# The FFN's down product by one level of Strassen's method, one product of halves at a time

## The chip, the core and the metric

The program runs on one core of one Trainium2 chip. The metric is the device time of one execution in microseconds, lower is better. The core has a matrix engine (PE, with its weight loads PEld), a vector engine (DVE), a scalar engine (ACT), a general engine (POOL) and a queue engine (SP); each works through its own list of instructions in order. DMAs are issued from SP's list (queue q1) and from POOL's list (queue q0).

## What is computed

One decoder layer for 1024 prompt rows and 64 sample rows with the same weights. The change concerns the last part, the convolutional feed-forward block:

```python
def conv_ffn(h, conv_buf, w_a, w_b, conv_w, conv_b, w_d):
    T = h.shape[1]
    a = h @ w_a                                    # (T, 4096)
    ctx = jnp.concatenate([conv_buf.astype(a.dtype), a], axis=1)
    c = conv_b
    for j in range(CONV_W):
        c = c + ctx[:, j:j + T] * conv_w[j]
    y = (jax.nn.silu(c) * (h @ w_b)) @ w_d         # (T, 4096) @ (4096, 1024)
    return y, ctx[:, -(CONV_W - 1):]
```

The result is normalised by row, scaled, and added to the residual. All values are float32 and the products have to be accurate, so each operand x is split into a high part (x rounded to fp32r) and a low part (the rest), and a product takes three matmuls: high with high, low with high, high with low.

## The kernel before, in words

The program is written with a tile framework that sets the order of the instructions on each engine before the run, from a simulated timeline; buffers come from pools, and an instruction that takes a buffer waits for its last reader.

**Stages.** Up to about 1630 us: attention, recurrence and the projections. From 1630 to 2337 us the up products (`up`, line 1609, and `ffn`, line 1653): the 4096 hidden columns go in 32 blocks of 128 (`fb`), two blocks at a time as a *pair*, 16 pairs. For a pair, `up` runs once for w_a and once for w_b, and it already uses the seven products of Strassen's method (Winograd's form, table `PRODS`): the 1024 model columns are the inner dimension in two halves, the two blocks are the two row halves, and the activation rows the two column halves. DVE makes the weight sums (line 1587), ACT and DVE the high and low parts (`split`, lines 143 and 144), and DVE and ACT take the results out of PSUM (lines 1635 to 1649, 1683 to 1685, 1705 to 1708). Between the two `up`s come the convolution (lines 1697 to 1699) and SiLU. The pair's hidden values stand in `ct`, tiles named `ext`, and POOL's queue writes them to memory (`yd`, lines 1711 and 1712), the 1024 prompt columns and the 64 sample columns of each block apart. In the same list POOL copies the convolution's tails (lines 1692 and 1693).

**The down product** (from 2337 us): `down_first` prepares blocks 0 and 1 during the last `up`; `down_group` (line 1769) then takes the blocks in groups: 1, 1, 2 and then seven groups of 4. For each of 8 row tiles of 128 prompt rows and each half of the 1024 output columns it runs 3 matmuls per block into a PSUM bank (line 1787) and adds the bank to an accumulator in SBUF (line 1793, DVE; for the first block lines 149 and 151). The sample rows' high and low parts are one 128-column stationary operand with 4 matmuls per block (line 1779). Each group's `w_d` rows and hidden values are loaded and split while the group before it runs (`prep`, line 1805; `down_part`, line 1735). In the last group each row tile is finished as soon as its sums are complete (`rows_done`, line 1818): residual loaded, row norm, scale, add, store.

**What sets the order around the change.** Six PSUM banks rotate in `down_bank`; PE's list is in program order up to what the simulated timeline moves; POOL's list carries the stores of the hidden values; SP's list carries all loads, and an SP entry that waits holds up those behind it.

Of the kernel before, what the change touches and what calls it, by code (L numbers as in the profile page):

```python
# [17 lines left out]
F32 = mybir.dt.float32  # L18
# [53 lines left out]
def _constants():  # L72
# [26 lines left out]
    for B in (2, 4, 8, 16, 32, 64):  # L99
# [7 lines left out]
RATES = (("prompt", 0.6), ("sample", 0.7), ("combine", 0.25))  # L107
RATE_INPUTS = 1.0
# [8 lines left out]
         ("S1", "T1", "C", True), ("A22", "T4", "B", False), ("S4", "B22", "C", False))  # L117


class Builder:  # L120
# [1265 lines left out]
    def phase3(self, early):  # L1386
# [3 lines left out]
        with ExitStack() as es:  # L1390
# [3 lines left out]
            self.yd = [self.dr.tile([P, NT], F32, name=f"yd{f}") for f in range(NFB)]  # L1394
# [258 lines left out]
    def ffn(self, es, eu, pool, fs, stT):  # L1653
# [5 lines left out]
        fp = pool(eu, "fp", 4)  # L1659
        W = SEQ + 2 + SB * 10  # L1660
# [9 lines left out]
        first_down = self.down_first(fp)  # L1670
        self.aside = chain(self.aside, first_down)
        for i in range(NFB // 2):
# [13 lines left out]
            self.up(store_a, i == 0)  # L1686
            ct = []
# [21 lines left out]
            self.up(store_b)  # L1709
            for m, fb in enumerate(fbs):  # L1710
                nc.gpsimd.dma_start(self.yd[fb][:, :SEQ], ct[m][:, 2:2 + SEQ])
                nc.gpsimd.dma_start(self.yd[fb][:, SEQ:].rearrange("p (b t) -> p b t", t=8), samples(ct[m])[:, :, 2:])
# [3 lines left out]
        for _ in range(2):  # L1716
            self.down_group([self.aready.popleft()])
        tails = fp.tile([P, W], F32, name="ext")
        o = 0
        for (j0, n, dst) in ((0, 2, O["p_ffn_conv"][0, 0]), (2, 16, O["s_ffn_conv"][0].rearrange("b j f -> (b j) f"))):  # L1720
            d2 = dst.rearrange("j (r p) -> (j r) p", p=P)
            for a in range(0, n, 4):
                w = min(4, n - a)
                ps = self.down_bank()
# [6 lines left out]
        self.down(es, pool)  # L1731
# [3 lines left out]
    def down_part(self, fb, raw, w, yraw, y, ys):  # L1735

        nc = self.nc
        nc.sync.dma_start(raw, self.I["w_ffn_d"][0][fb * P:(fb + 1) * P])
        nc.sync.dma_start(yraw, self.yd[fb])
        self.split(*w, raw)  # L1740
        self.split(*y, yraw[:, :SEQ])
        self.split(ys[:, 0], ys[:, 1], yraw[:, SEQ:])
        return w, y, ys.rearrange("p a b -> p (a b)")

    def wtile(self, pool, name, dt=F32R, bufs=2):
        return pool.tile([P, 8, P], dt, name=name, bufs=bufs).rearrange("p a f -> p (a f)")

    def down_first(self, fp):

        for fb in range(2):  # L1750
            w = [self.wtile(self.wp, n) for n in ("w_hi", "w_lo")]
            y = [self.wtile(self.uw, *n) for n in ((("wx", F32R, 3), ("wx", F32R, 3)), (("wx", F32R, 3), ("w_raw", F32R, 1)))[fb]]
            yraw = fp.tile([P, SEQ + 2 + SB * 10], F32, name="ext")[:, :NT]
            ys = self.uw.tile([P, 4, P], F32R, name="S", bufs=3)[:, 0].rearrange("p (a b) -> p a b", a=2)
            yield self.down_part(fb, self.wtile(self.wp, "w_raw", F32), w, yraw, y, ys)

    def down_start(self, pc):
        self.pc, self.nb = pc, 0
        accs = [self.actp.tile([P, 4, D], F32, name=f"act_{x}0") for x in "hl"]
        self.acc = [accs[i // 4][:, i % 4] for i in range(SEQ // P)]  # L1760
        self.smp = [pc.tile([P, 512], F32, name="ps_c") for _ in range(2)]
        self.ndown = 0

    def down_bank(self, n=6):
        pl, nm = [(self.pd, "ps_d"), (self.pu, "ps_u"), (self.pc, "ps_c")][(self.nb // 2) % (n // 2)]
        self.nb += 1
        return pl.tile([P, 512], F32, name=nm)

    def down_group(self, grp, after=lambda i: None, sampled=lambda: None):

        nc = self.nc
        G = len(grp)
        first = self.ndown == 0
        self.ndown += G
        last = self.ndown == NFB
        for k, (w, _, ys) in enumerate(grp):
            for u in range(2):
                for x in range(2):
                    nc.tensor.matmul(self.smp[u], ys, w[x][:, u * 512:(u + 1) * 512], start=first and k + x == 0, stop=last and k + x == G)  # L1779
        sampled()  # L1780
        for i, acc in enumerate(self.acc):
            for u in range(2):
                ps = self.down_bank()
                m = 0
                for w, y, _ in grp:
                    for a, b in ((0, 0), (1, 0), (0, 1)):
                        nc.tensor.matmul(ps, y[a][:, i * P:(i + 1) * P], w[b][:, u * 512:(u + 1) * 512], start=m == 0, stop=m == 3 * G - 1)  # L1787
                        m += 1
                dst = acc[:, u * 512:(u + 1) * 512]
                if first:  # L1790
                    self.copy(dst, ps)
                else:
                    nc.vector.tensor_add(dst, dst, ps)
            after(i)

    def down(self, es, pool):
# [3 lines left out]
        nc.sync.dma_start(gb, I["norm_ffn_post"][0].partition_broadcast(P))  # L1800
        sel = dp.tile([P, NS], F32, name="sel")
        nc.vector.tensor_add(sel, self.ident[:, :NS], self.ident[:, NS:])
        held = {}

        def prep(g, j, fb):

            if g % 2 == 0:
                if j == 0:
                    held[g] = [self.actp.tile([P, 4, D], F32R, name=f"act_{x}1") for x in "hl"]
                y = tuple(t[:, j] for t in held[g])  # L1810
            else:
                y = tuple(dp.tile([P, D], F32R, name=n, bufs=4) for n in ("yh", "yl"))
            w = (self.wtile(self.wp, "w_hi"), self.wtile(self.wp, "w_lo")) if g % 2 == 0 and j < 2 else \
                tuple(dp.tile([P, D], F32R, name="wd", bufs=12) for _ in range(2))
            ys = dp.tile([P, 2, NS], F32R, name="ys", bufs=9)
            return self.down_part(fb, self.wtile(self.wp, "w_raw", F32), w, dp.tile([P, NT], F32, name="y_raw", bufs=2), y, ys)

        def rows_done(src, rows, r0, dst):

            x, y = (dp.tile([P, D], F32, name=n, bufs=4)[:rows] for n in ("yh", "yl"))  # L1820
            nc.sync.dma_start(x, self.x1d[r0:r0 + rows])
            ss = self.sm.tile([P, 2], F32, name="pn_ss")[:rows]
# [3 lines left out]
            r = self.rstd(ss[:, 0:1], rows, D)  # L1826
            for u in range(2):
                v = slice(u * 512, (u + 1) * 512)
                nc.vector.scalar_tensor_tensor(y[:, v], src(u), r, gb[:rows, v], op0=ALU.mult, op1=ALU.mult)
                nc.vector.tensor_add(y[:, v], y[:, v], x[:, v])  # L1830
                nc.sync.dma_start(dst[:, v], y[:, v])

        def samples_done():
            s = [dp.tile([P, 512], F32, name=f"smp{u}") for u in range(2)]
            fin = []
            for u in range(2):
                nc.scalar.activation(s[u], self.smp[u], AF.Copy)
                ps = self.down_bank(4)[:NS]
                nc.tensor.matmul(ps, sel, s[u], start=True, stop=True)
                fin.append(ps)  # L1840
            rows_done(lambda u: fin[u], NS, SEQ, O["y_sample"].rearrange("b t d -> (b t) d"))
        groups = [(2, 3)] + [tuple(range(a, a + 4)) for a in range(4, NFB, 4)]
        grp = [prep(1, j, fb) for j, fb in enumerate(groups[0])]
        for g, _ in enumerate(groups, 1):
            nxt = []
            todo = deque(groups[g] if g < len(groups) else ())

            def after(i):
                for _ in range(1 if len(grp) == 4 else 2):
                    if i % 2 == 0 and todo:  # L1850
                        nxt.append(prep(g + 1, len(nxt), todo.popleft()))
                if g == len(groups):
                    acc = self.acc[i]
                    rows_done(lambda u: acc[:, u * 512:(u + 1) * 512], P, i * P, O["y_prompt"][0, i * P:(i + 1) * P])
            self.down_group(grp, after, samples_done if g == len(groups) else lambda: None)
            grp = nxt
# [31 lines left out]
```

## Time and profile before

| | |
|---|---|
| median of 3 runs | 2749.05 us (2740.54, 2749.05, 2750.15) |
| the profiled execution | 2738.69 us, its span 2736.8 us |
| PE busy | 2640.7 us, 96% of the span |
| DVE busy | 1659.2 us, 61% |
| ACT busy | 1085.8 us, 40% |
| POOL busy | 196.8 us, 7% |
| HBM read, written | 302.07 MB, 123.46 MB |

The busy time of an engine is the union of its instructions' times, so that neighbours that overlap count once. A wait stands with the instruction that waited and what ended it. Windows are in us from the start of the span.

### The profile page before, as it was taken

The page shows a single profiled execution, that of the slowest core. Times are in us where ns is not written, and L with a number is a line of the kernel's source. Part 1 is how long each engine was busy: PE and PEld are TensorE (multiplying, and loading weights), DVE is VectorE, ACT ScalarE, POOL GpSimd, SP SyncE. Part 2 cuts the span into 40 slices and gives each one's busy share as a digit, 9 for nine tenths or more (in the row PEclk, how much of TensorE's full clock was granted, in tenths as well). Part 3 has the DMA queues.
Part 4 walks back from the last instruction along what each step waited for, and adds up shares of the span by engine and source line. Part 5 has one row for each costly group of instructions (what it writes and reads, how often), then busy time and mean ns, then how long its engine had stood idle before and what let it go on. Part 6 is the DMA issues. An engine that isn't in the chain of part 4 may idle for free.

```text
span 2736.8 us, 45512 instructions
## 1 busy us (share of the span) xinstructions
PE 2640.7 (96%) x17822; PEld 2387.3 (87%) x17822; DVE 1659.2 (61%) x3981; ACT 1085.8 (40%) x2000; POOL 196.8 (7%) x339
## 2 busy tenths in 40 slices
PE   7999999999999999999999998999999999999998
PEld 6988888887888988989989877999999999788886
DVE  7346657657656745454447577777677676843536
ACT  5224526435346544444422464333333334311212
POOL 2100010010011000000000000000000100000000
PEclk9999999999999999999999998999999999999999
DMA  7456676867767322232376442332332332521303
GB/s 230 129 180 183 184 224 185 214 194 182 207 191 193 109 95 94 87 102 83 105 249 220 173 139 76 115 110 98 113 117 78 98 98 72 186 97 64 127 32 131
DMA packets 344551, 380.72 MB, mean 139 GB/s; under 512 B 57067, under 2 KB 295075, under 8 KB 343416
## 3 DMA queue, kind: packets, MB, share of 16 engines
q1 hardware_dynamic: 321808, 311.13, 37.9%
q0 software_dynamic: 22240, 65.63, 7.5%
q8 instruction: 140, 2.29, 0.3%
q10 hardware_dynamic: 288, 1.05, 0.1%
q14 instruction: 75, 0.61, 0.1%
HBM read 302.07 MB, written 123.46 MB: 155 GB/s over the span
## 4 chain that ended last, share of the span: by engine, by line
PE 82%; DMA 6%; issue 6%; DVE 3%; ACT 2%; SPq 1%; POOL 0%; DVEq 0%; POOLq 0%; ACTq 0%
PE ps_d L244 32%; PE ps_u L1630 10%; PE ps_c L1630 7%; PE ps_d L1630 7%; PE ps_u L1787 4%; PE ps_d L1787 4%; PE ps_c L1787 4%; DMA qb<-qrow 2%; PE ps_d L1428 1%; PE ps_u L1428 1%; DMA kt<-kb 1%; PE ps_c L1779 1%; PE ps_n L1428 1%; PE ps_sc L1226 1%; DMA qrow<-qn 1%
## 5 line engine op out<-in xcount | busy, mean ns | idle before, releaser
L244 PE MATMUL ps_d<-act_h,w_hi 128*128 128x512 f32 (+2 forms) x1920 | 647.2, 337 | 5.6 <-DVE proj L832 5.0
L244 PE MATMUL ps_d<-act_l,w_hi 128*128 128x512 f32 (+2 forms) x1920 | 648.0, 338 | 0.0
L244 PE MATMUL ps_d<-act_h,w_lo 128*128 128x512 f32 (+2 forms) x1920 | 643.7, 335 | 0.0
L244 PEld LDWEIGHTS ps_d<-act_h,w_hi 128*128 128x128 f32 x1920 | 366.2, 191 | 33.9 <-DVE proj L832 5.7
L244 PEld LDWEIGHTS ps_d<-act_l,w_hi 128*128 128x128 f32 x1920 | 366.0, 191 | 30.1 <-issue 3.9
L244 PEld LDWEIGHTS ps_d<-act_h,w_lo 128*128 128x128 f32 x1920 | 365.8, 191 | 27.4 <-issue 2.5
L143 ACT ACTIVATE w_hi<-w_raw 128x1024 fp32r<-128x1024 f32 (+1 forms) x156 | 140.5, 902 | 294.7 <-PE ps_d L244 187.8
L144 DVE TENSOR_TENSOR w_lo<-w_raw,w_hi 128x1024 fp32r<-128x1024 f32 (+1 forms) x124 | 138.3, 1117 | 118.2 <-ACT w_hi L143 116.8
L1066 DVE CUSTOM_DVE_ANT_0 qb<-kc,qb 128x128 f32<-128x128 f32 x384 | 89.1, 286 | 100.2 <-DMA qb<-qrow 86.5
L1630 PE MATMUL ps_u<-Yh,w_hi 128*128 128x288 f32 (+1 forms) x512 | 103.7, 291 | 5.6 <-ACT Yh L143 5.6
L1630 PE MATMUL ps_c<-Yh,wx 128*128 128x288 f32 (+1 forms) x512 | 107.6, 292 | 0.0
L1630 PE MATMUL ps_d<-act_h,w_lo 128*128 128x288 f32 (+1 forms) x512 | 102.5, 290 | 3.8 <-ACT uT L1635 3.8
L1630 PE MATMUL ps_u<-act_h,w_lo 128*128 128x288 f32 (+1 forms) x512 | 104.8, 288 | 0.9 <-DVE u L1638 0.9
L1630 PE MATMUL ps_u<-Yh,wx 128*128 128x288 f32 (+1 forms) x512 | 103.0, 290 | 2.5 <-DVE u L1643 2.5
L1630 PE MATMUL ps_d<-act_h,w_hi 128*128 128x288 f32 (+1 forms) x512 | 102.8, 290 | 0.1
L1630 PE MATMUL ps_c<-act_h,wx 128*128 128x288 f32 (+1 forms) x512 | 101.4, 288 | 0.0
L244 PE MATMUL ps_d<-ohi,w_hi 128*128 128x256 f32 (+2 forms) x288 | 95.0, 331 | 3.1 <-ACT proj L1144 2.0
L244 PE MATMUL ps_d<-olo,w_hi 128*128 128x320 f32 (+2 forms) x288 | 95.2, 331 | 0.0
L244 PE MATMUL ps_d<-ohi,w_lo 128*128 128x320 f32 (+2 forms) x288 | 94.8, 330 | 0.0
L143 ACT ACTIVATE wx<-S 128x512 fp32r<-128x512 f32 x64 | 40.4, 632 | 126.9 <-PE ps_c L1630 124.3
L1144 ACT ACTIVATE proj<-ps_d,nbin 128x512 f32<-128x512 f32 (+2 forms) x96 | 53.2, 554 | 94.4 <-PE ps_d L244 94.2
L1630 PEld LDWEIGHTS ps_u<-Yh,w_hi 128*128 128x128 f32 x512 | 83.6, 192 | 5.8 <-ACT Yh L143 5.8
(639 smaller groups left out, 6299.2 us busy)
## 6 DMA issues: line engine op xcount, KB each, us to landing
w_raw<-in_w_in SPq DMA_DIRECT2D x80, 512.0 KB, 4.0
out_s_win<-in_cache_win_kv SPq DMA_DIRECT2D x40, 1016.0 KB, 7.1
kc<-in_cache_win_kv SPq DMA_DIRECT2D x80, 256.0 KB, 3.9
qb<-qrow SPq DMA_DIRECT2D x64, 256.0 KB, 4.9
kc<-in_cache_win_kv SPq DMA_DIRECT2D x128, 128.0 KB, 3.5
w_raw<-in_w_ffn_a SPq DMA_DIRECT2D x32, 512.0 KB, 3.8
w_raw<-in_w_ffn_b SPq DMA_DIRECT2D x32, 512.0 KB, 3.6
yd<-ext POOLq DMA_DIRECT2D x32, 512.0 KB, 4.7
```

The source lines that it names most:

```text
L143: self.nc.scalar.activation(hi, src, AF.Copy)
L144: self.nc.vector.tensor_sub(lo, src, hi.bitcast(F32))
L244: nc.tensor.matmul(ps, W[:, c], X(c), start=n == 0, stop=n == 3 * kb - 1)
L1066: nc.vector.tensor_tensor_reduce(q[:, j], k[:, j], q[:, j], 1.0, 0.0, ALU.mult, ALU.add, T[:, c:c + 1])
L1144: self.proj(col, lambda ps, a, e: nc.scalar.activation(y[:, a:e], ps, AF.Exp, bias=nb, scale=-1.0))
L1226: nc.tensor.matmul(ps[:, j * P:(j + 1) * P], E[:, c:c + P], E[:, c:c + P], start=True, stop=True)
L1428: mm = nc.tensor.matmul(ps[u], mg[x][:, k, o:o + e - a], wk[k][w][:, u * 512:(u + 1) * 512], start=k == m == 0, stop=k == (6 if i == 8 els ...
L1630: nc.tensor.matmul(p, w[:, c], self.side_b(t, b, x, c), start=new and m == 0, stop=m == 11, skip_group_check=not new)
L1779: nc.tensor.matmul(self.smp[u], ys, w[x][:, u * 512:(u + 1) * 512], start=first and k + x == 0, stop=last and k + x == G)
L1787: nc.tensor.matmul(ps, y[a][:, i * P:(i + 1) * P], w[b][:, u * 512:(u + 1) * 512], start=m == 0, stop=m == 3 * G - 1)
```

## The change

The down product becomes seven products of halves instead of eight. The hidden columns are the inner dimension: the two blocks of a pair are its two halves. The prompt rows 0 to 511 and 512 to 1023 are the row halves, output columns 0 to 511 and 512 to 1023 the column halves. The products run **one after the other over all 16 pairs** (table `DOWN`): a product keeps four PSUM banks, one for each 128 of its 512 rows, over 16 pairs; products that are added to one another go on in the same banks. Between products the banks are copied or added into the four quarters of the output (`down_sums`).

The sums that the products need are made beforehand, in the up stage. `weight_sums` runs three times for each pair (176, 176 and 160 columns of each half): POOL's queue loads the two blocks' `w_d` columns, DVE makes four differences, POOL's queue stores them (`wq`). After the second `up` DVE makes the pair's four sums of hidden values, and POOL's queue stores seven half-width arrays (`yq`). The samples stay outside Strassen's method: their hidden values go to one array (`ysd`), loaded and split once at the start of the down stage, and their matmuls ride along with the four products whose weights are plain `w_d` sums.

In the down stage one step is one pair of one product: two loads of 256 KB (`down_load`), one split of both (high by ACT, low by DVE), 12 matmuls. Three steps (`READY`) are prepared during the last `up`.

```diff
+YARR = ("A11", "S3", "A12", "A22", "S1", "S2", "S4")
+QROUNDS = ((0, QW), (QW, 2 * QW), (2 * QW, 512))
+DOWN = (("S2", "T2", True), ("S3", "T3", False), ("A22", "T4", False), ("A11", "B11", True), ("A12", "B21", False),
+        ("S1", "T1", True), ("S4", "B22", False))
+READY = 3
+LAST = 8
...
+        def weight_sums(i, a, e):
+
+            w = qp.tile([P, 4, QW], F32, name="wq")[:, :, :e - a]
+            for j in range(2):
+                nc.gpsimd.dma_start(w[:, 2 * j:2 * j + 2], I["w_ffn_d"][0][(2 * i + j) * P:(2 * i + j + 1) * P]
+                                    .rearrange("p (u f) -> p u f", u=2)[:, :, a:e])
+            nc.vector.tensor_sub(w[:, 0], w[:, 1], w[:, 0])
+            nc.vector.tensor_sub(w[:, 1], w[:, 3], w[:, 1])
+            nc.vector.tensor_sub(w[:, 3], w[:, 3], w[:, 0])
+            nc.vector.tensor_sub(w[:, 2], w[:, 2], w[:, 3])
+            nc.gpsimd.dma_start(self.wq[i][:, :, a:e], w)
...
             self.up(store_a, i == 0)
+            weight_sums(i, *QROUNDS[0])
...
+            weight_sums(i, *QROUNDS[1])
             self.up(store_b)
+            weight_sums(i, *QROUNDS[2])
+            A = [[ct[m][:, 2 + 512 * t:514 + 512 * t] for m in range(2)] for t in range(2)]
+            q = qp.tile([P, 3, 512], F32, name="q")
+            nc.vector.tensor_add(q[:, 0], A[1][0], A[1][1])
+            nc.vector.tensor_sub(q[:, 1], q[:, 0], A[0][0])
+            nc.vector.tensor_sub(A[1][0], A[0][0], A[1][0])
+            nc.vector.tensor_sub(q[:, 2], A[0][1], q[:, 1])
...
+            nc.gpsimd.dma_start(flat(4, 3), q.rearrange("p a f -> p (a f)"))
             for m, fb in enumerate(fbs):
-                nc.gpsimd.dma_start(self.yd[fb][:, :SEQ], ct[m][:, 2:2 + SEQ])
-                nc.gpsimd.dma_start(self.yd[fb][:, SEQ:].rearrange("p (b t) -> p b t", t=8), samples(ct[m])[:, :, 2:])
+                nc.gpsimd.dma_start(flat(2 * m, 2), ct[m][:, 2:2 + SEQ])
+                nc.gpsimd.dma_start(self.ysd[:, fb].rearrange("p (b t) -> p b t", t=8), samples(ct[m])[:, :, 2:])
...
+    def down_group(self, s, p0, steps, after=lambda i: None):
+        new = DOWN[s][2]
+        for i in range(4):
+            if new and p0 == 0:
+                self.dbank[i] = self.down_bank()
+            ps = self.dbank[i]
+            for j, (yh, yl, wh, wl) in enumerate(steps):
+                p = p0 + j
+                for m, (y, w) in enumerate(((yh, wh), (yl, wh), (yh, wl))):
+                    nc.tensor.matmul(ps, y[:, i * P:(i + 1) * P], w, start=new and p + m == 0, stop=p == NPAIR - 1 and m == 2,
+                                     skip_group_check=not new)
+            if p0 + len(steps) == NPAIR:
+                self.down_sums(s, i, ps)
             after(i)
...
+        def prep(n):
+            nonlocal count
+            while len(ready) < n and todo:
+                s, p = todo.popleft()
+                raw = self.halves(self.wp, raws[count % len(raws)], F32)
+                self.down_load(raw, s, p)
+                nm, b = slots[count % len(slots)]
+                count += 1
+                st = dp.tile([P, 2, 2, 512], F32R, name=nm, bufs=b)
+                self.split(st[:, 0], st[:, 1], raw)
+                ready.append((st[:, 0, 0], st[:, 1, 0], st[:, 0, 1], st[:, 1, 1]))
...
+                elif s == 1 and p == 2:
+                    ysr = self.actp.tile([P, NFB, NS], F32, name="act_l1")
+                    nc.sync.dma_start(ysr, self.ysd)
+                    ys = self.actp.tile([P, NFB, 2, NS], F32R, name="act_h1")
+                    for f in range(0, NFB, 8):
+                        self.split(ys[:, f:f + 8, 0], ys[:, f:f + 8, 1], ysr[:, f:f + 8])
```

In the built lists the down stage has 1344 matmuls for the prompt (line 1822 of the changed kernel; 1536 before, line 1787) and 128 for the samples (line 1919; 128 before, line 1779). Up to the second half of pair 0 all five engines' lists are as before. Three places differ as follows.

DVE, second `up` of a pair in the middle of the up stage. `u_...<-ps_u` frees a PSUM bank that PE writes next; `wq` is the buffer of `weight_sums`. Before:

```order
L1699 SCALAR_TENSOR_TENSOR ext<-ext,fvec 128x1104
L1638 TENSOR_TENSOR u_20495<-ps_u,uT 128x288
L1677 MEMSET ext 128x2
L1691 COPY ext<-stT 128x8x2
L144 TENSOR_TENSOR w_hi<-S,w_hi 128x512
L1708 TENSOR_TENSOR ext<-ps_d,ext 128x256
```

and now:

```order
L1727 SCALAR_TENSOR_TENSOR ext<-ext,fvec 128x1104
L1694 TENSOR_TENSOR wq<-wq 128x160
L1653 TENSOR_TENSOR u_21218<-ps_u,uT 128x288
L1704 MEMSET ext 128x2
L1719 COPY ext<-stT 128x8x2
L157 TENSOR_TENSOR w_hi<-S,w_hi 128x512
L1736 TENSOR_TENSOR ext<-ps_d,ext 128x256
```

The first difference of a weight round, which waits for that round's loads, has come to stand directly ahead of the instruction that frees a bank.

POOL, the end of the last pair and the start of the down stage (`q` holds three sums of hidden values; `ysd` the samples):

```order
L1749 DMA yq_16103<-ext 128x1024
L1750 DMA ysd<-ext 128x8x8 x2
L1749 DMA yq_16103<-ext 128x1024
L1747 DMA yq_16103<-q 128x1536
L1767 DMA out_p_ffn_conv<-ext 64x128
```

The sample values of the last pair are stored behind the first block's hidden values; before, the same place held two pairs of `yd` stores.

ACT at the start of the down stage (`w_lo` and `wx` are the last of the three steps made ahead, `sa`, `sb` and `sc` the split steps that follow):

```order
L156 ACTIVATE w_lo<-w_raw 128x512 x2
L156 ACTIVATE wx<-w_raw 128x512 x2
L156 ACTIVATE act_h_25947<-act_l_25945 128x8x64 x4
L156 ACTIVATE sa<-w_raw 128x1024 x2
L156 ACTIVATE sa<-w_hi 128x1024
```

The four splits of all sample values, which need the load of `ysd`, have come to stand ahead of the first split of the fourth step; before, ACT went on there with evictions and the blocks' own splits.

## Rows read from the trace of the kernel before

**Rows 1.** The page's busy times: busy us, share of the span, instructions.

```profile
PE 2640.7 (96%) x17822; PEld 2387.3 (87%) x17822; DVE 1659.2 (61%) x3981; ACT 1085.8 (40%) x2000; POOL 196.8 (7%) x339
```

**Rows 2.** Windows: length, busy us and count per engine, granted clock, DMA share, GB/s.

```profile
1700.00:2331.00 631.00, 631.00 (x5027) 631.00 (x5027) 456.91 (x967) 230.34 (x376) 55.15 (x120) 1.00 0.32 101
2331.00:2405.00 74.00, 70.84 (x327) 57.85 (x327) 59.00 (x92) 28.47 (x40) 5.58 (x9) 1.00 0.57 183
2405.00:2675.00 270.00, 270.00 (x1180) 221.06 (x1179) 112.03 (x153) 45.16 (x60) 0.00 (x0) 1.00 0.23 76
```

**Rows 3.** The chain of work in order of time, down stage: start, length, matmuls.

```profile
2400.86 5.57 PE ps_u L1787 x24
...
2448.87 5.44 PE ps_d L1787 x24
```

**Rows 4.** DVE's timeline inside one pair: start, length, instruction, idle before.

```profile
2017.07 0.52 DVE L1685 TENSOR_TENSOR ext<-ps_u,uT 128x256 f32<-128x256 f32 x2 [0.57 <-PE ps_u L1630]
...
2028.17 0.45 DVE L1638 TENSOR_TENSOR u<-ps_u,uT 128x288 f32<-128x288 f32 x1
...
2036.65 0.68 DVE L1587 TENSOR_TENSOR S<-w_raw 128x512 f32<-128x512 f32 x1
```

**Rows 5.** PE's timeline in that pair: the matmul that reuses the freed bank.

```profile
2031.61 0.30 PE L1630 MATMUL ps_u<-act_h,w_lo 128*128 128x288 f32 x1
```

**Rows 6.** POOL's DMA issues of lines 1711 and 1712: issue ns, landing us, min/median/max.

```profile
L1711 POOL DMA_DIRECT2D yd<-ext x32: 549/550/581, 1704.8 to 2338.4; - x32
...
DMA to landing us min/median/max: 3.0/4.7/8.3
...
L1712 POOL DMA_DIRECT2D yd<-ext x32: 901/903/912, 1705.4 to 2339.0; - x32
...
DMA to landing us min/median/max: 3.3/5.2/8.9
```

**Rows 7.** PE's timeline at the start of the down stage.

```profile
2336.82 0.29 PE L1630 MATMUL ps_c<-act_h,wx 128*128 128x288 f32 x1
...
2362.55 0.50 PE L1787 MATMUL ps_d<-wd,yh 128*128 128x512 f32 x1 [1.32 <-ACT yh L143]
...
2366.06 0.51 PE L1787 MATMUL ps_d<-wd,yl 128*128 128x512 f32 x1 [1.84 <-DVE yl L144]
```

**Rows 8.** Landing times: the page's DMA issues, and those of the down stage.

```profile
out_s_win<-in_cache_win_kv SPq DMA_DIRECT2D x40, 1016.0 KB, 7.1
...
w_raw<-in_w_ffn_d SPq DMA_DIRECT2D x28, 512.0 KB, 4.6
...
yh<-x1d SPq DMA_DIRECT2D x1, 256.0 KB, 3.4
```

**Rows 9.** The page's split groups: busy us, mean ns of one.

```profile
L143 ACT ACTIVATE w_hi<-w_raw 128x1024 fp32r<-128x1024 f32 (+1 forms) x156 | 140.5, 902 | 294.7 <-PE ps_d L244 187.8
L144 DVE TENSOR_TENSOR w_lo<-w_raw,w_hi 128x1024 fp32r<-128x1024 f32 (+1 forms) x124 | 138.3, 1117 | 118.2 <-ACT w_hi L143 116.8
...
L143 ACT ACTIVATE wx<-S 128x512 fp32r<-128x512 f32 x64 | 40.4, 632 | 126.9 <-PE ps_c L1630 124.3
```

**Rows 10.** Windows of PE alone: length, busy (count), granted clock, DMA share, GB/s.

```profile
1668.00:1670.00 2.00, 0.00 (x0) 0.67 0.00 0
1670.00:1672.00 2.00, 1.29 (x5) 0.50 0.00 0
...
1674.00:1676.00 2.00, 2.00 (x12) 0.62 0.04 8
...
2364.00:2366.00 2.00, 0.21 (x1) 1.00 0.68 132
```

**Rows 11.** PE's last matmul and DVE's last instructions, from their timelines.

```profile
2725.05 0.39 PE L1787 MATMUL ps_c<-wd,act_h 128*128 128x512 f32 x1
...
2728.04 0.15 DVE L1825 TENSOR_TENSOR pn_ss<-pn_ss 128x1 f32<-128x1 f32 x1
...
2731.93 1.29 DVE L1830 TENSOR_TENSOR yl<-yl,yh 128x512 f32<-128x512 f32 x2
```

More of the change, by code (lines that the diff above doesn't have):

```diff
@@ L107 @@
 RATES = (("prompt", 0.6), ("sample", 0.7), ("combine", 0.25))
+QW = 176
 RATE_INPUTS = 1.0
@@ L1659, in ffn @@
         fp = pool(eu, "fp", 4)
+        qp = pool(eu, "qp", 1)
         W = SEQ + 2 + SB * 10
@@ L1730, in ffn, with down_load @@
         eu.close()
-        self.down(es, pool)
-    def down_part(self, fb, raw, w, yraw, y, ys):
+        self.down(es, pool, steps[2:])
+    def down_load(self, raw, s, p):
         nc = self.nc
[L1738 to L1755, printed above, removed]
+        y, w, _ = DOWN[s]
@@ new lines, in down_load, with halves, down_first @@
+        nc.sync.dma_start(raw[:, 0], self.yq[p][:, YARR.index(y)])
+        if w[0] == "T":
+            src = self.wq[p][:, WARR.index(w)]
+        else:
+            fb, u = 2 * p + int(w[1]) - 1, int(w[2]) - 1
+            src = self.I["w_ffn_d"][0][fb * P:(fb + 1) * P, u * 512:(u + 1) * 512]
+        nc.sync.dma_start(raw[:, 1], src)
+    def halves(self, pool, name, dt=F32R, bufs=2):
+        return pool.tile([P, 8, P], dt, name=name, bufs=bufs).rearrange("p (a b) f -> p a (b f)", a=2)
+    def down_first(self):
+        k = 0
+        for p in range(READY):
+            raw = self.halves(self.wp, "w_raw", F32)
+            self.down_load(raw, 0, p)
+            for x in range(2):
+                pl, nm, bufs = self.slots[k]
+                k += 1
+                t = self.halves(pl, nm, F32R, bufs)
+                self.split(t[:, 0], t[:, 1], raw[:, x])
+                yield t
@@ L1757, in down_start @@
     def down_start(self, pc):
         self.pc, self.nb = pc, 0
[L1759 to L1765, printed above, removed]
+        self.acc = [self.actp.tile([P, 4, 2, 512], F32, name=f"act_{x}0") for x in "hl"]
@@ L1766, in down_bank @@
+        self.dbank = {}
+    def down_bank(self):
+        pl, nm = [(self.pd, "ps_d"), (self.pu, "ps_u"), (self.pc, "ps_c")][(self.nb // 2) % 3]
         self.nb += 1
         return pl.tile([P, 512], F32, name=nm)
-    def down_group(self, grp, after=lambda i: None, sampled=lambda: None):
+    def down_group(self, s, p0, steps, after=lambda i: None):
         nc = self.nc
[L1772 to L1793, printed above, removed]
-            after(i)
@@ new lines, in down_sums @@
+    def down_sums(self, s, i, ps):
+        nc = self.nc
+        (c11, c12), (c21, c22) = ([a[:, i, u] for u in range(2)] for a in self.acc)
+        copy = lambda dst: nc.scalar.activation(dst, ps, AF.Copy)
+        if s < 3:
+            copy((c12, c22, c21)[s])
+        elif s == 3:
+            copy(c11)
+            nc.vector.tensor_add(c12, c12, c11)
+            nc.vector.tensor_add(self.acc[1][:, i], self.acc[1][:, i], c11.unsqueeze(1).to_broadcast([P, 2, 512]))
+        elif s == 4:
+            copy(c11)
+        else:
+            c = c22 if s == 5 else c12
+            nc.vector.tensor_add(c, c, ps)
@@ L1797, in down @@
+    def down(self, es, pool, steps):
         tc, nc, I, O = self.tc, self.nc, self.I, self.O
@@ L1818, in rows_done @@
[L1818 to L1822, printed above, removed]
+        snap, *smps = (dp.tile([P, 512], F32, name=f"smp{u}") for u in range(3))
+        slots = 3 * [("sa", 3)] + 3 * [("sc", 3)] + 4 * [("sb", 4)]
+        for n, b in (slots[0], slots[-1], slots[3]):
+            dp.tile([P, 2, 2, 512], F32R, name=n, bufs=b)
@@ L1823, in rows_done @@
+        rows = 0
+        def rows_done(src, n, r0, dst):
+            nonlocal rows
+            x, y = (xy[:n, 2 * (rows % 2) + j] for j in range(2))
+            rows += 1
+            nc.sync.dma_start(x, self.x1d[r0:r0 + n])
+            ss = self.sm.tile([P, 2], F32, name="pn_ss")[:n]
             for u in range(2):
@@ L1840, in samples_done @@
                 fin.append(ps)
             rows_done(lambda u: fin[u], NS, SEQ, O["y_sample"].rearrange("b t d -> (b t) d"))
[L1842 to L1856, printed above, removed]
+        smp = {}
```

80 lines of the change are left out of this document (53 added, 27 removed).

## The prediction, made before the changed kernel was run

> **What bounds the kernel now.** I read the page's busy times first: PE is busy for 96% of the span, no other engine for more than 61% [rows 1]. That is an average, so the next view is the windows of the two stages that the change touches [rows 2]. From 1700 to 2331 us PE is busy for all 631 us, DVE for 456.91 (72%). The same holds from 2405 to 2675. Only the stretch between, 2331 to 2405, has PE idle: 74 - 70.84 = 3.2 us. So a matmul that is left out is worth its full length, and work added elsewhere is free until somebody makes PE wait. The clock was at the higher level, 2.4 GHz (1.00), in all three.
>
> The chain of work in order of time gives the price of a matmul: blocks of 24 take 5.57 or 5.44 us [rows 3], 0.2321 or 0.2267 us each, mean 0.2294.
>
> **The matmuls left out.** The lists have 1344 instead of 1536 prompt matmuls and the same 128 for the samples. 192 x 0.2294 = **-44.0 us** (43.5 by the shorter pitch, 44.6 by the longer).
>
> **Their pitch.** The two pitches alternate with the pool that holds the operands; the shorter belongs to groups whose operands all stand in `dp`, as those of all but three of the new steps do. All 1344 at 0.2267 instead of the mean: -3.6; all at the longer: +3.6. I take **-2**, more than half of the way to the nearer case.
>
> **The up stage.** For each of 16 pairs DVE gets 12 differences of 128x176 or 160 and 4 of 128x512. The nearest row is a 128x512 sum in SBUF at 0.68 us [rows 4]. By width a difference takes 0.68 x 176/512 = 0.23, at most the 0.45 of the 128x288 there. Per pair that is 12 x 0.23 + 4 x 0.68 = 5.5 us (8.1 at most). A pair takes 631 us / 5027 matmuls x 336 = 42.2 us and DVE works 0.72 x 42.2 = 30.6 of them, so it goes to 36 to 39 us, 86 to 92%. It still fits.
>
> What matters is where the work stands. In the order of DVE's list the first difference of a round stands right ahead of the addition that frees a bank (2028.17 in the pair shown). This difference waits for a chain on POOL's queue: after the last difference of the round before (at about 2018, by the evictions at 2017.07) its store must be issued and land, as there is one buffer `wq`, then two loads must be issued and land. A POOL issue takes 0.55 us with long pieces and 0.90 with short ones, and lands after 4.7 to 5.2 us, 3.0 at the least [rows 6]. At the medians 0.6 + 4.7 + 1.2 + 4.7 = 11.2 us; with the low landings 7.8. There are about 10 us, so at the medians DVE is 1.2 us late. But PE takes up the freed bank only at 2031.61 [rows 5], 3.0 us after the addition's end at 2028.62. That cover swallows it. I take **+2 us** for the whole stage, for single late rounds; the bounds are 0 and 24 (1.5 us in every pair). If the cover goes, the wait shows on PE at the matmul that reuses a bank.
>
> POOL itself gets 14 issues for 4 per pair, at most 14 x 0.9 = 12.6 of 42.2 us: its queue is not full. On this queue lie the loads, ahead of the stores of hidden values, which nobody needs before the down stage.
>
> The Trainium skill has a rule against putting more DMAs on this queue. Its page "SBUF — State Buffer", section "SBUF: two separate sides", says that the descriptors of a DMA issued from GpSimd cannot be written while DVE runs an operation that holds the port they share, and gives about 620 ns alone and 3100 ns beside a copy. In this trace, with DVE 72% busy, 32 issues ran from 549 to 581 ns [rows 6], so nothing of it shows. If each issue did take 3.1 us, the three issues in the chain would add an estimated 7.5 us to it; the sum does not use this.
>
> **The turn to the down stage.** Call S the end of the last up matmul, 2336.82 + 0.29 = 2337.1 [rows 7]. PE has three prepared steps of 12 matmuls and some transposes: 36 x 0.2321 + 0.4 = 8.8 us, until S+8.8. The fourth step (`sa`) is not there. In ACT's list its split stands behind the four sample splits, which need `ysd`, whose last store POOL can issue only after the last pair's values are final, at about S+1.9 (the last store of line 1712 before, at 2339.0). Landing 5.2, S+7.1. Then the 1 MB load: between the 4.6 us of 512 KB and the 7.1 of 1016 KB [rows 8]; I take 6.0, nearer to the row of its size, since only one is under way: S+13.1. Four sample splits at 0.63 and the first of `sa` at 0.90 on ACT [rows 9]: S+16.5. DVE's low half (1.12) ends 1.1 us later; in PE's list four matmuls that need only the high half come first and cover 0.9 of it. So PE stands idle for 16.5 - 8.8 = 7.7 us, 7.9 with the rest of the low half, in place of the 1.32 + 1.84 = 3.2 us that it loses now at 2362 to 2366 [rows 7]: +4.7. With landing 3.3 and load 4.6 it is +1.4, with 8.9 and 7.1 it is +9.5.
>
> An idle PE can also lose its clock. After PE stood idle at 1668 the granted clock was 0.67, then 0.50 (1.2 GHz) at 1670, still 0.62 in 1674 to 1676 [rows 10]: some 6 us near half speed, 2.8 us lost. In 2364 to 2366, with one matmul in 2 us, it stayed at 1.00. The new gap has no matmul at all and resembles the first row, so I add 2.5 (0 to 3). The turn is **+7 us**, between +1.4 and +12.5.
>
> **The steps themselves.** A step is 12 x 0.2294 = 2.75 us of PE; ACT needs 0.90 and DVE 1.12 for its splits [rows 9], both hidden. Its two loads of 256 KB in 2.75 us are 190 GB/s; now the stretch 2331 to 2405 ran at 183 with a DMA share of 0.57 [rows 2]. A load of this size lands after 3.4 us [rows 8], and six raw buffers give a step some 16 us of lead: hidden. The evictions of the old accumulation go, all but a few, which helps DVE and no one else.
>
> **Product boundaries.** Between products a bank must be copied out before it is written again; six banks rotate and four are in use, so the first two new banks are free and the others have had 5 us. After the sixth product DVE normalises four row tiles (per tile two multiplications and two additions at about 0.65 each, as at 2731.93 [rows 11], and small ones: some 4 us, 16 in all) and makes the splits of the last eight steps (8 x 1.12 = 9): 25 us beside the last product's first half, 8 x 2.75 + samples = 26 us. This is tight; **+3** (0 to 12).
>
> **The end.** Now the last matmul starts at 2725.05 and the span ends at 2736.8; DVE comes to the last tile's sum (`pn_ss`, 2728.04) behind the sixth tile's work [rows 11]. In the new list the last tile is 5.5 us behind the one before it, as now, but only one addition per tile is left. **-1.5** (-2.5 to +3).
>
> **The sum.** -44.0 - 2 + 2 + 7 + 3 - 1.5 = -35.5 us. On the profiled execution, 2738.69 us, that is 2703.2. The median of the runs is 10.4 us above it (2749.05), so the forecast is 2713.6, **2714 us**.
>
> **The rivals.**
>
> *The turn and the boundaries cost their upper bounds.* +12.5 instead of 7 and +12 instead of 3: +14.5, **2728 us**. For it speaks that everything hangs on one load behind one store; against it, the medians [rows 6, 8]. Chance 0.12.
>
> *DVE becomes late in the up stage.* At 92% any burst is carried over. If PE loses 1 to 2 us in each pair instead of 2 us in all, it is +14 to +30: **2728 to 2744 us**. The 3.0 us of cover in the pair shown [rows 4, 5] speaks against it; that I looked at one place of three rounds speaks for it. Chance 0.10.
>
> *Slower: the weight rounds are late on POOL's queue.* If the two landings take the 8.3 us of the slowest store [rows 6], the chain is 0.6 + 8.3 + 1.2 + 8.3 = 18.4 us instead of 10; DVE stands for 8.4, and after 3.0 of cover PE for 5.4 us per pair: 16 x 5.4 = 86, less the 2 in the sum, **2798 us**. It decides from (35.5 + 2)/16 = 2.3 us of PE loss per pair: there the gain is gone. For it speaks one buffer and one queue; against it, the median of 4.7. Chance 0.04.
>
> *Slower: transfers bound the down stage.* If the loads of 256 KB ran one after another at 3.4 us [rows 8], 218 of them would take 741 us instead of 340. The 183 GB/s with 43% left [rows 2] speaks against it. **3110 us**, chance 0.02.
>
> *The change doesn't save the matmuls.* The lists show the 1344; what is open is only a longer pitch, within the bounds. No more than 0.01 for no change.
>
> **How the numbers follow.** The forecast has 0.71. Its own bounds: the lower ends together (-44.6 - 3.6 + 0 + 1.4 + 0 - 2.5 = -49.3) give 2700, and the runs of before reach 8.5 below their median, so I set the low end at 2695. The high end, 2738, takes in the first rival and most of the second. A measurement of this kernel can tell about 0.5%, 13.7 us, so faster means under 2735.3: 0.71 + 0.12 and half of the second rival, 0.88, less 0.02 for the forecast's own upper tail: 0.86. Same 0.08, slower 0.06.
>
> **What would show it right or wrong.** The down stage should last about 350 us instead of 388, with one gap on PE of 7 to 8 us that begins 9 us after its start and ends on ACT's split of `sa`, behind the sample splits that wait for `ysd`; the granted clock falls after it. In the up stage DVE is at 86 to 92%, PE waits for next to nothing, and POOL's issues stay at 0.55 to 0.9 us. A PE wait that returns three times in a pair, ending on a DVE eviction behind a difference that waited for its load, would make the forecast wrong; so would PE waits on split steps throughout the down stage.

## The result, and the profile after

| | before | changed |
|---|---|---|
| median | 2748.81 us (2740.54 to 2750.15, 4 runs) | 2706.07 us (2703.72 to 2708.28, 4 runs) |
| profiled execution's span | 2736.8 us | 2705.9 us |
| DVE busy in 1700 to 2331 | 456.91 us | 531.49 us |

The ratio is 0.9852, with a 95% interval of 0.9836 to 0.9868: 42.7 us less at the medians. The forecast was 2714, 35 us less, in a range of 2695 to 2738. The time lies in the range, and more was gained than was forecast.

The two spans differ by only 30.9 us, so the first thing to read is where. PE's timelines of the two kernels, first matmul of the up stage of before:

```profile
1633.55 0.28 PE L1630 MATMUL ps_d<-act_h,w_hi 128*128 128x256 f32 x1
```

and of the changed kernel: the first of the up stage, the first of the down stage, and the two around the one long gap (start, length, in brackets the wait):

```profile
1644.79 0.28 PE L1645 MATMUL ps_d<-act_h,w_hi 128*128 128x256 f32 x1
...
2349.43 0.86 PE L1822 MATMUL ps_d<-w_hi 128*128 128x512 f32 x3
...
2358.08 0.27 PE L1763 MATMUL ps_c<-ident,tail 128*128 128x128 f32 x1
2364.92 1.22 PE L1822 MATMUL ps_d<-sa 128*128 128x512 f32 x2 [6.57 <-ACT sa L156]
```

The changed kernel's execution is 11.2 us late already at the start of the up stage, where nothing was changed yet. In the eleven profiled executions of this study that matmul starts anywhere from 1632.85 to 1644.90. The profiled execution of before was an early one, which is why the prediction added 10.4 us to come from it to the median. From the start of the up stage on, the parts are:

- Up stage: 2337.19 - 1633.55 = 703.6 us before, 2349.43 - 1644.79 = 704.6 now: **+1.0**. Five of the experiments below leave the code of the up stage as it is, and there it took 702.4 to 704.9 us, so this difference is inside the scatter.
- Down stage, to PE's last matmul: 2337.19 to 2725.44 before [rows 11], 388.3; now 2349.43 to 2696.71, 347.3: **-41.0**.
- From there to the end: 11.4 us before, 9.2 now: **-2.2**.

Together -42.2, which agrees with the medians' 42.7. The page of the changed kernel answers to [rows 1]:

```profile
PE 2599.8 (96%) x17632; PEld 2355.2 (87%) x17632; DVE 1707.5 (63%) x4124; ACT 1137.0 (42%) x2036; POOL 318.9 (12%) x499
```

Its windows answer to [rows 2]:

```profile
1700.00:2331.00 631.00, 629.23 (x5008) 628.56 (x5007) 531.49 (x1215) 229.08 (x374) 172.72 (x273) 1.00 0.53 170
...
2375.00:2405.00 30.00, 30.00 (x134) 24.86 (x133) 20.16 (x17) 19.00 (x20) 0.00 (x0) 1.00 0.91 320
2405.00:2675.00 270.00, 270.00 (x1186) 221.89 (x1185) 124.17 (x135) 104.93 (x133) 0.00 (x0) 1.00 0.55 175
```

and its windows of PE alone to [rows 10]:

```profile
2360.00:2362.00 2.00, 0.00 (x0) 0.95 1.00 328
2362.00:2364.00 2.00, 0.00 (x0) 0.50 0.96 329
2364.00:2366.00 2.00, 1.08 (x3) 0.50 1.05 406
2366.00:2368.00 2.00, 2.00 (x6) 0.50 1.08 412
2368.00:2370.00 2.00, 2.00 (x9) 0.84 1.02 408
```

Up stage: PE misses 1.8 us, DVE is at 84%. Turn: the clock is at 1.2 GHz (0.50) from 2362 to 2368, and PE works there from 2364.92 on: 3.08 us at half speed and 2 at 0.84 lose 1.9 us. After that PE is busy throughout. In the chain of work in order of time the pitch is 2.72 us for 12 matmuls from end to end, 0.2267 each; the chain leaves PE for the turn alone:

```profile
2354.79 6.86 DMA act_l<-ysd
2362.27 1.65 ACT act_h L156 x3
2364.92 1.22 PE ps_d L1822 x2
...
2375.12 2.72 PE ps_d L1822 x12
...
2489.37 0.93 PE ps_c L1919 x4
```

ACT's timeline tells the same of the turn, 14.42 us idle for the load of `ysd`:

```profile
2361.73 2.19 ACT L156 ACTIVATE act_h<-act_l 128x512 fp32r<-128x512 f32 x4 [14.42 <-DMA act_l<-ysd]
2363.83 1.99 ACT L156 ACTIVATE sa<-w_raw 128x1024 fp32r<-128x1024 f32 x2
```

The two splits of `sa` from `w_raw` are the fourth and the fifth step. SP's timeline shows that the loads of both were issued early, and that the load of `ysd`, which had to wait for the last store, held up only those of the sixth (`w_hi`) and later ones:

```profile
2348.28 0.32 SPq L1777 DMA_DIRECT2D w_raw<-yq  x1
...
2354.79 0.32 SPq L1933 DMA_DIRECT2D act_l<-ysd  x1
2355.16 0.42 SPq L1777 DMA_DIRECT2D w_hi<-yq  x1
```

### The profile page after: what moved, and what is told of

Its sections match the earlier page's. It is cut to its first block, busy times and chain, and to the rows that moved or that the text cites. A ratio compares the mean times of both kernels' runs of the same rounds, so it can differ in the third digit from the quotient of the medians.

```text
span 2705.9 us, 45915 instructions
## 1 busy us (share of the span) xinstructions
PE 2599.8 (96%) x17632; PEld 2355.2 (87%) x17632; DVE 1707.5 (63%) x4124; ACT 1137.0 (42%) x2036; POOL 318.9 (12%) x499
## 4 chain that ended last, share of the span: by engine, by line
PE 76%; DMA 9%; issue 7%; DVE 3%; ACT 2%; SPq 2%; POOL 1%; DVEq 0%; POOLq 0%; ACTq 0%
PE ps_d L257 29%; PE ps_u L1645 10%; PE ps_c L1645 7%; PE ps_d L1645 7%; PE ps_d L1822 4%; PE ps_u L1822 4%; PE ps_c L1822 3%; DMA qb<-qrow 2%; DMA kt<-kb 1%; PE ps_d L1443 1%; PE ps_u L1443 1%; PE ps_c L1919 1%; PE ps_n L1443 1%; DMA kc<-in_cache_win_kv 1%; PE ps_sc L1239 1%
## 5 line engine op out<-in xcount | busy, mean ns | idle before, releaser
L156 ACT ACTIVATE w_hi<-w_raw 128x1024 fp32r<-128x1024 f32 (+1 forms) x148 | 131.4, 888 | 200.8 <-PE ps_d L257 187.3
L157 DVE TENSOR_TENSOR w_lo<-w_raw,w_hi 128x1024 fp32r<-128x1024 f32 (+1 forms) x114 | 126.5, 1110 | 112.9 <-ACT w_hi L156 112.2
```

The source lines that it names most:

```text
L156: self.nc.scalar.activation(hi, src, AF.Copy)
L157: self.nc.vector.tensor_sub(lo, src, hi.bitcast(F32))
```

## The experiments

All are edits of the changed kernel, and their times stand beside its 2706.07 us and ratio 0.9852; each ratio is against runs of before on the same chip.

### The turn: the splits later, and the load too

```diff
-                elif s == 1 and p == 2:
+                elif s == 1 and p == 10:
...
+                    with tc.issue_after(moved["act"].ins), tc.issue_after(moved["dve"].ins):
                         for f in range(0, NFB, 8):
                             self.split(ys[:, f:f + 8, 0], ys[:, f:f + 8, 1], ysr[:, f:f + 8])
```

`moved` holds the last step's two split instructions and its last load; `issue_after` puts what follows behind them in the same engine's list. `turn_both` does the same to the load, with `moved["sp"]`.

> The four sample splits stand some twenty steps later in ACT's and DVE's lists; the load of ysd stays where it is in SP's list. Theory 1 (the order in the splitting engines' lists makes the gap of 6.57 us at the turn): the fourth step is split as soon as its own load has landed, so the gap before it goes. The fifth step's loads were issued only behind the load of ysd (2355.16, landing 6.6 us later), so a gap of 2 to 3 us is left there; the clock stays at the higher level. Time: 5 to 7 us less than the changed kernel's 2706, about 2700. Theory 2 (the fourth step's own load is late): the gap stays at 5 us or more, 2705 to 2706.

> As turn_splits, and the load of ysd too stands some twenty steps later in SP's list. Theory 1 (the order of the lists makes the gap, SP's included): no PE wait over 1 us at the turn, granted clock 1.00 throughout, the gap of 6.57 us and some 2.4 us of half clock come back: 9 us less than the changed kernel, about 2697. Theory 2 (steps are late by themselves at the turn, for loads in a burst land late): PE waits of 3 us or more stay somewhere in the first twenty steps, 2700 to 2706.

`turn_splits`: 2700.55 us, ratio 0.9831 (0.9815 to 0.9847), 5.5 us under the changed kernel. `turn_both`: 2696.9 us, ratio 0.9812 (0.9794 to 0.9829), 9.2 us under it. PE's waits at the turn in `turn_both`:

```profile
PE ps_d L1822 <- DVE sa L157: 2.0, 1, 2.0
```

In both the gap of 6.57 us is gone: ACT splits the fourth step before the down stage begins (at 2345.65 in `turn_splits`, at 2342.95 in `turn_both`). So the order of ACT's and DVE's lists made the gap, as theory 1 said. The 9.2 us agree with theory 1 partly by luck: only 6.3 of them lie in the down stage, PE's first to last matmul (341.0 us instead of 347.3), where theory 1 had counted 9; the rest is inside the scatter of the other stages.

What the load's place in SP's list is worth by itself isn't shown. The down stage of `turn_splits` took 342.7 us, 1.7 more than that of `turn_both`, and 1.7 us is what `turn_splits` lost to the clock, which fell behind its wait (windows in the last section). The wait that was expected at the fifth step did not come, for those loads were never behind that of `ysd`: the expectation took the sixth step's loads for the fifth's.

The expected "no wait over 1 us" was missed: 2.0 us are left, for another reason that DVE's timeline of `turn_both` shows. The small addition `sel` waits for the store of `q`, and the low split of the fourth step stands behind it:

```profile
2355.56 0.23 DVE L1930 TENSOR_TENSOR sel<-ident 128x64 f32<-128x64 f32 x1 [1.15 <-DMA yq<-q]
2355.70 2.35 DVE L157 TENSOR_TENSOR sa<-w_raw,sa 128x1024 fp32r<-128x1024 f32 x2
```

In `turn_splits` a wait of 2.07 us stood at the same place. No run moves `sel` alone; in `combo` below, where the pool `dp` is laid out otherwise, `sel` doesn't wait, and 0.7 us are left.

### The up stage: no weight rounds, more differences, a longer chain

`no_rounds` returns from `weight_sums` at once. `twice_diff` and `half_diff` repeat all four differences, or the last two; `read_back` adds one DMA:

```diff
             nc.gpsimd.dma_start(self.wq[i][:, :, a:e], w)
+            nc.gpsimd.dma_start(w, self.wq[i][:, :, a:e])
```

> Leaves out all 48 weight rounds (loads, differences, stores); the products whose weights are differences take plain halves of w_ffn_d in their place, so the loads of the down stage are the same in number and size. Theory 1 (the rounds are hidden, up to the 1.3 us that PE waits longer on DVE in the up stage): 0 to 3 us less than the changed kernel, 2703 to 2706. Theory 2 (they cost PE time in ways that its waits do not show, by contention): 8 us less or more, under 2698.

> Does the four differences of each round twice in place, 192 more on DVE at 0.335 us: 4.0 us more in each pair, DVE at 94% of the up stage instead of 84%; the values of the differences are others. Theory 1 (DVE's idle time of 6.6 us per pair takes it, as PE is ahead of no wait): 0 to 5 us more than the changed kernel, 2706 to 2711. Theory 2 (DVE is already at the edge, for it is needed at fixed places): 1 to 2 us per pair, 2722 to 2738.

> Repeats two of the four differences of each round: 2.0 us more on DVE per pair, half of twice_diff's addition; the values of the differences are others. The lists show the last round inside the last pair, where twice_diff has three rounds behind the up stage. Theory 3 (twice_diff's 35 us came from rounds that slipped behind the up stage, one chain of store, load, differences after the other, and not from DVE's busy time): 0 to 5 us more than the changed kernel, 2706 to 2711. Theory 2 (DVE's busy time, in proportion): some 17 us more, 2720 to 2726.

> After each weight round POOL's queue reads the stored round back into the same buffer, before the next round's loads may start: one issue of 0.7 us and one landing of about 3 us more in the chain of each of the 48 rounds, nothing more on DVE or PE. The lists show four rounds behind the last pair's stores, as twice_diff's do three, with their differences ahead of the first low splits of the down stage in DVE's list. Theory 3 (the chain of the rounds is what runs short, and where it is late the rounds slip behind the up stage): the up stage grows by 0 to 4 us, and PE stands at the turn on DVE's split of the fourth step, 25 to 45 us in all: 2731 to 2751. The slower rival of the prediction (a late round holds DVE and so PE in every pair): the up stage itself grows by 30 us or more. Theory 4 (the chain has room for 4 us per round): 2706 to 2711.

| kernel | median, us | ratio (interval) | up stage, us | PE's long waits at the turn, us | last difference ends, us |
|---|---|---|---|---|---|
| changed | 2706.07 | 0.9852 (0.9836 to 0.9868) | 704.6 | 6.6 | -39.6 |
| no_rounds | 2704.03 | 0.9842 (0.9827 to 0.9858) | 701.9 | 6.8 | none |
| half_diff | 2715.82 | 0.9895 (0.9882 to 0.9909) | 709.3 | 8.5 | +8.6 |
| twice_diff | 2741.56 | 0.9979 (0.9967 to 0.9991) | 706.3 | 15.9 + 21.3 | +46.8 |
| read_back | 2810.39 | 1.0236 (1.0211 to 1.0261) | 760.1 | 16.2 + 39.4 | +66.8 |

The up stage is counted from its first matmul to the first of the down stage; the last column gives the end of the last round's differences on DVE, counted from there, and shows how far the rounds have slipped.

`no_rounds` agrees with theory 1: all of the 48 rounds cost 2 us, which is within the uncertainty, and at most 2.7 us of up stage, which is no more than the scatter.

`twice_diff` fell outside both of its theories. The time, 35 us more, suits the second, but the up stage grew by only 1.7 us. What was lost stands at the turn, in PE's waits of `twice_diff`:

```profile
PE ps_d L1823 <- DVE sa L157: 21.3, 1, 21.3
PE ps_d L1823 <- ACT sa L156: 15.9, 1, 15.9
```

and in its POOL timeline:

```profile
2366.76 1.44 POOL L1692 DMA_DIRECT2D wq<-in_w_ffn_d  x2 [7.60 <-DMA wq<-wq]
2375.17 0.74 POOL L1699 DMA_DIRECT2D wq<-wq  x1 [6.97 <-DVE wq L1698]
2378.32 1.41 POOL L1692 DMA_DIRECT2D wq<-in_w_ffn_d  x2 [2.42 <-DMA wq<-wq]
```

The last rounds run one after the other behind the up stage, and their differences stand ahead of the first low splits in DVE's list. That is the wait of 21.3 us, and theory 3 was made from it. The 15.9 us are the gap of the changed kernel grown longer: ACT's split of the fourth step stands behind the sample splits there too, and the load of `ysd`, issued 10.3 us after the first matmul of the down stage behind eight other loads, took 11.2 us to land (5.4 and 6.9 us in the changed kernel).

`half_diff` was made to test theory 3 and decides little. It cost 10 us, between theory 3's bound of 5 and theory 2's 17. Its last round does slip, but only to the turn. The wait of 8.5 us there is not the changed kernel's: in `half_diff` the sample splits stand behind six splits of steps, and DVE's low split of the fourth step stands behind `sel`, which waits for the store of `q` (late in part because DVE had stood 3.5 us for the last round's loads, ahead of the sums in `q`):

```profile
2369.28 0.23 DVE L1932 TENSOR_TENSOR sel<-ident 128x64 f32<-128x64 f32 x1 [7.64 <-DMA yq<-q]
```

Its up stage took 709.3 us, above the scatter, with waits of PE of 4.8 us from 1700 on (1.8 in the changed kernel). That DVE's added work makes them is not shown: `twice_diff` adds twice as much, and its up stage grew by 1.7 us only.

`read_back` puts nothing on DVE and cost 104 us, more than any theory had said. Theory 3 was right about the turn but too low (waits of 55.6 us replace 6.6), and it had left the up stage at 4 us more; that grew by 55.5 us (3.5 per pair), past the mark of 30 set for the slower rival. PE's waits in `read_back` from 1630 us on:

```profile
PE ps_d L1823 <- DVE sa L157: 39.4, 1, 39.4
PE ps_d L1645 <- ACT uT L1650: 18.8, 8, 3.9
PE ps_d L1823 <- ACT sa L156: 16.2, 1, 16.2
PE ps_u L1645 <- DVE u L1653: 14.4, 9, 3.5
PE ps_u L1645 <- DVE u L1658: 12.7, 9, 2.6
```

DVE's waits for the rounds' loads from 1630 us to the end of the up stage:

```profile
DVE wq L1694 <- DMA wq<-in_w_ffn_d: 117.6, 42, 7.3
```

and PE alone from 1700 to 2400:

```profile
1700.00:2400.00 700.00, 660.88 (x5134) 0.98 0.53 170
```

Both mechanisms are there at once: rounds that slip behind the stage, and DVE held at fixed places by late loads (129 us with the 11.6 of line 1695, 8.1 per pair). PE stands idle for 700 - 660.88 = 39.1 us of the stretch shown, where the changed kernel's windows miss 1.8. The granted clock, 1.00 in the changed kernel, is 0.98 on the mean here: six times it fell to 0.50 behind a wait of PE, for 24 us in all, which cost some 11 us more. This is the prediction's slower rival, brought about by 4.3 us more in the chain (0.78 of issue, 3.5 of landing at the medians). The first wait at the turn, 16.2 us, is again the load of `ysd`, which landed 23.4 us after the first matmul of the down stage; the second, 39.4 us, is the rounds. In the changed kernel DVE waits in all 25.5 + 2.6 us for the rounds' loads, and its POOL rows give the chain:

```profile
L1692 POOL DMA_DIRECT2D wq<-in_w_ffn_d x96: 708/712/752, 1682.3 to 2303.2; - x96
...
DMA to landing us min/median/max: 2.7/3.0/8.7
...
L1698 POOL DMA_DIRECT2D wq<-wq x48: 723/737/767, 1687.8 to 2310.8; - x48
...
DMA to landing us min/median/max: 2.8/3.6/6.9
```

0.74 + 3.6 + 1.42 + 3.0 = 8.8 us where the prediction had 11.2 from the rows of other stores [rows 6]. It fits into the 10 us, and 4.3 us more do not. Beside a DVE at 84% the issue of 512 KB of hidden values takes 574 ns at the median, where it took 550 at 72%, and no DMA that POOL issues from 1640 us on takes more than 1003 ns. So the price of 3100 ns that the Trainium skill gives ("SBUF — State Buffer", section "SBUF: two separate sides") shows nowhere in this trace. The page doesn't expect it here either: it has that price beside a `tensor_copy`, and says of `tensor_tensor`, which most of DVE's work in the up stage is, that it did not stall such DMAs.

### The down stage: its transfers, and the pitch

`two_of_three` leaves out one of three matmuls:

```diff
-                for m, (y, w) in enumerate(((yh, wh), (yl, wh), (yh, wl))):
+                for m, (y, w) in enumerate(((yh, wh), (yh, wl))):
```

> Leaves out the matmuls of the low part of the hidden values (448 of 1344); loads, splits and everything else stay. A step is then 8 matmuls, 1.81 us, and its two loads of 256 KB make 290 GB/s instead of 193. Theory 1 (PE is the bound of the down stage and the transfers have room up to the 320 GB/s seen at a DMA share of 0.91): 448 x 0.2267 = 102 us less than the changed kernel, 2604 to 2612. Theory 2 (the transfers are near their bound at the changed kernel's rate of 175 to 190 GB/s): little is gained, PE waits on split steps all through the stage, 2660 or more.

2609.02 us, ratio 0.9506 (0.9493 to 0.952): 97 us less, as expected of theory 1. The down stage is 101 us shorter (246.3 instead of 347.3); the time from PE's last matmul to the end grew from 9.2 to 16.9 us. Its windows, all engines:

```profile
2405.00:2575.00 170.00, 170.00 (x744) 139.10 (x743) 112.01 (x125) 92.26 (x121) 0.00 (x0) 1.00 0.75 246
```

PE is still busy for all of it, at 246 GB/s and a DMA share of 0.75. The transfers do not bound the changed kernel at 175.

> Two places change and nothing else: the first two of the steps made ahead have the hidden values in pool wp and the weights in pool uw (both in one of them before), and the samples' operand stands in pool dp, with the weights, instead of actp. Theory 1 (a matmul takes 0.2267 us when both operands come from one pool, 0.2333 us when they come from two): the first 24 matmuls of the down stage go up to 0.2333 each, the samples' matmuls of line 1919 go down from 0.2333 to 0.2267. Theory 2 (the pitch depends on the stationary operand's place alone): the first 24 stay at 0.2267. Time within 2 us of the changed kernel.

The edit gives the first two steps their buffers in another order and moves `ys` to `dp`. PE's timeline of `pools` at the start of the down stage:

```profile
2347.99 2.50 PE L1822 MATMUL ps_d<-wx,w_hi 128*128 128x512 f32 x10
2350.33 0.39 PE L1822 MATMUL ps_u<-wx,w_hi 128*128 128x512 f32 x1
```

Ten matmuls take 2350.33 - 2347.99 = 2.34 us, 0.234 each; in the changed kernel the same matmuls stand 2.72 us for 12 apart. In the chain of `pools` the samples' four stand as

```profile
2490.24 0.91 PE ps_c L1920 x4
```

against 0.93 us in the changed kernel (2489.37 above). Both went the way of theory 1: 0.227 with both operands from one pool, about 0.233 from two. What about the pools does it (their place in memory, say) is open.

`pools` ran once, at 2701.35 us, below its range of 2 us around the changed kernel. With `ys` from another pool its splits came to stand behind six splits of steps in ACT's list, which was not intended, and the gap of 6.57 us became three short ones (1.5, 0.9 and 0.8 us). That is a third look at the same cause.

### All that helped, together

The edits of `turn_both`, `ys` in `dp` as in `pools`, and one matmul fewer at the end, which alone is shown:

```diff
-                nc.scalar.activation(smps[u], smp[u], AF.Copy)
+                if u:
+                    nc.vector.tensor_add(smps[u], snap, smp[u])
+                else:
+                    nc.scalar.activation(smps[u], smp[u], AF.Copy)
...
-                nc.tensor.matmul(ps, sel, smps[u], start=True, stop=u == 0)
-                if u:
-                    nc.tensor.matmul(ps, sel, snap, start=False, stop=True)
+                nc.tensor.matmul(ps, sel, smps[u], start=True, stop=True)
```

> turn_both, and besides the samples' operand in pool dp (0.9 us less if the matmuls of line 1919 take 0.2267) and one fp32 matmul fewer at the end (DVE adds the two sums of the samples; 1.0 us less). By the theory that the list order made the gap: 2 us less than turn_both's 2697, about 2695. The rival (nothing there is on the path): 2697.

2690.5 us, ratio 0.9808 (0.9789 to 0.9827). The interval holds `turn_both`'s ratio of 0.9812, so the time does not tell the two apart. The trace does: the down stage is 337.9 us instead of `turn_both`'s 341.0, of which 1.2 is the wait for the low split (0.7 left of 2.0) and 1.8 what remains for the two edits, expected to bring 1.9. Of the versions that leave nothing out it has the lowest median, 1.9% under the kernel before.

## Why the prediction was right

- **The matmuls and their pitch** (-44.0 and -2). Right, and a little small. Of the 41.0 us that the down stage lost, the turn took 5.3 and a third fp32 matmul for the samples 1.0, so -47.3 is what is left for matmuls and pitch. The pitch of the prompt's matmuls is 0.2267 throughout, the lower bound of that term. The reason given was too narrow: not `dp`, but one pool for both operands, whichever it is.
- **The up stage** (+2, DVE at 86 to 92%). Measured +1.0, inside the scatter, DVE at 84%. The differences take 0.33 us, more than the 0.23 taken for them. The chain of a round was over-estimated, 11.2 against 8.8 us. The view that the place of the waiting difference matters, more than DVE's share, is borne out: `read_back` adds nothing on DVE and cost 104 us, which also shows how near the edge the chain was.
- **The turn** (+7, idle 7.7 to 7.9, clock 2.5). Measured: idle 6.57, clock 1.9, less the 3.2 that before lost: +5.3. The mechanism is the one named, and `turn_splits` shows it. Counted from S, the end of the last up matmul, here 2349.59: PE's work ended at S+8.8 (forecast S+8.8), the sample load was issued at S+5.2 (forecast S+7.1) and landed 6.9 us later (forecast 6.0), and PE went on at S+15.3 (forecast S+16.5). That the sum came so near has some luck in it, for the early issue and the slow load offset one another. The clock's 2.8 us were misread: in the stretch of [rows 10] PE was idle for part of the time at half speed, and lost 2.4.
- **Product boundaries** (+3). This term was wrong: PE waits for nothing after the turn. All that came was a third fp32 matmul for the samples at the end, the one that `combo` takes out, 1 us, which the prediction did not have.
- **The end** (-1.5). Measured -2.2.
- **The rivals.** The turn cost less than its upper bound and the boundaries nothing. DVE late in the up stage, slow rounds and transfers as the bound did not come. The slow rounds need 4.3 us more of chain, and the transfers were no bound at 246 GB/s. (By its own figures the rival with the transfers is 2713.6 + 741 - 340 = 3115 us, not 3110.)

The sum was -35.5, the parts came to -42.2. All terms erred to the same side: the boundaries by 2.0 (3.0, less the third fp32 matmul), the turn by 1.7, matmuls and pitch by 1.3, the up stage by 1.0, the end by 0.7.

## What to carry to other kernels

Where PE is the bound, matmuls saved are worth their pitch, and the open questions are the places where lists meet: look in each engine's list at what stands ahead of the first work of the new stage, and at what that waits for. Preparation that rides in another stage has two limits, its engine's busy time and its own chain through one buffer; the second can run out first, and much of the loss may show up only at the stage's end, where the late work stands ahead of the next stage's first.

## What was not expected of the hardware

The same matmul took 0.227 us with both operands from one pool and about 0.233 with operands from two, 3%, in both directions of the test.

The clock after a short idle stretch of PE is not settled by the length of that stretch alone. After 2.07 us in `turn_splits` it fell, after 1.96 us in `turn_both` it did not. `turn_splits`, PE alone:

```profile
2358.00:2360.00 2.00, 0.22 (x1) 1.00 0.95 335
2360.00:2362.00 2.00, 2.00 (x7) 0.72 1.01 366
2362.00:2364.00 2.00, 2.00 (x6) 0.50 1.04 389
```

and `turn_both`:

```profile
2356.00:2358.00 2.00, 1.03 (x4) 1.00 1.03 351
2358.00:2360.00 2.00, 2.00 (x10) 1.00 1.05 404
```

These two lengths are nearly the same, so by themselves they decide nothing. `read_back` does: after 3.25 us the clock stayed, and after 1.76 us it fell. PE's timeline and its windows there:

```profile
1860.55 0.38 PE L1645 MATMUL ps_u<-act_h,w_lo 128*128 128x256 f32 x1 [3.25 <-DVE u L1653]
...
1860.00:1862.00 2.00, 1.45 (x12) 1.00 0.26 57
1862.00:1864.00 2.00, 2.00 (x16) 1.00 1.02 373
...
2304.50 0.39 PE L1645 MATMUL ps_u<-Yh,wx 128*128 128x256 f32 x1 [1.76 <-DVE u L1658]
...
2306.00:2308.00 2.00, 2.00 (x11) 0.51 0.52 180
2308.00:2310.00 2.00, 2.00 (x13) 0.63 0.00 0
```

What decides it is open.
